# Transposing q and k in fp32, two row tiles at a time, and splitting them into halves behind the transposes

## The chip, the cores and the metric

The kernel runs on one core of a Trainium2 chip. The metric is the device time of one execution in microseconds (us). The core's engines are PE (TensorE, matrix products, with weight loads shown apart as PEld), DVE (VectorE), ACT (ScalarE), POOL (GpSimd) and SP (SyncE, which here only issues transfers). Each engine runs its own queue in order; engines wait for one another through semaphores. Matmul results are written to PSUM, which has eight banks; DVE and ACT read them from there.

## What is computed

An encoder trunk of two layers on 512 rows of 1024 channels, in fp32. Each layer normalises x, projects it (w_in) to q, k and v of two attention branches and to gates, and mixes:

```python
qa = apply_rope(rms_norm(qa.reshape(b, s, HEADS_A, 2, HEAD_DIM), qk_gain_a[l, 0]), cos, sin)
ka = apply_rope(rms_norm(ka.reshape(b, s, HEADS_A, 2, HEAD_DIM), qk_gain_a[l, 1]), cos, sin)
oa = diff_attention(qa, ka, va, lam)             # 8 heads, two softmaxes each, w = p0 - lam * p1
qb = apply_rope(rms_norm(qb...)); kb = ...       # 12 heads in 3 groups of dilated windows
ob = softmax-weighted sum of the three groups' dilated_window_attention
y = (g_a * (oa @ w_branch_a[l]) + g_b * (ob @ w_branch_b[l])) @ w_out[l]
x = x + gate_m * y
h = rms_norm(x, norm_mlp_g[l]) * (1.0 + scale_f) + shift_f
x = x + gate_f * (jnp.square(jax.nn.relu(h @ w_mlp_up[l])) @ w_mlp_down[l])
```

## The kernel before

Products are made in fp32r, a shortened fp32: each fp32 operand is split into a high half (its value rounded to fp32r) and a low half (what is left), and three matmuls (high by high, high by low, low by high) take the place of one. Weight halves are called wh and wl: `split_w` loads `raw`, ACT copies it to wh, and DVE subtracts to get wl.

The 512 rows are four row tiles of 128. The w_in columns are cut into 14 pieces; piece p holds 128 columns each of q, k and v, that is two heads of 64. Pieces 0 to 5 belong to branch B, pieces 6 to 13 to the eight heads of branch A. The main loop runs over slots: slot k multiplies row tile k%4 of piece k//4 (24 matmuls of 384 columns, in three parts, into an `acc` bank), and slots 56 to 61 multiply gates. Between the parts of a slot stands the work of earlier tiles and of attention, written out by hand in the loop (line 836 on). In that loop every engine's order is fixed as the code emits it (`Ordered`, `nosync`). For one row tile of one piece the steps are:

- `post1`, at the start of the next slot: ACT squares (sq) and copies v; DVE sums (ms), multiplies by gain and rotation (y, sw); POOL makes the scale (rs) and applies it to y, a tile of 128x256: q of two heads, then k of two heads.
- `post2`, at the end of the same slot: ACT writes the high halves of q and twice those of k into a tile T of 128x768 (fp32r), and DVE subtracts to get the low halves.
- `turn`, in the middle of slot k+2 (for the first 18 tiles at the start of slot k+3): PE transposes four 128x128 blocks of T into a PSUM bank tp; ACT copies them to q2 and k2.
- `turn_kl`, behind part 2 of that slot: PE transposes T's last block into the free columns of the slot's acc bank; ACT copies its lower 64 partitions to kl and DVE its upper 64.

Per head, q2 holds high and low half on the two partition halves, k2 the high half twice, and kl the low half on one side and zeros on the other, so a score is two matmuls:

```python
matmul(o, q2[:, c, qt], k2[:, c, ks], start=True, stop=False)
matmul(o, q2[:, c, qt], kl[:, c, ks], start=False, stop=True)
```

Attention B has its tiles in slots 14 to 17 and 26 to 29, two to a slot; a tile's e is transposed one slot later (six transposes tp<-e in two banks, copied by ACT to wT). Attention A has head h's four tiles in slots 30+4h to 33+4h. In such a slot, in this order: post1 of the slot before; `leave` (ACT, squares and copies of an earlier head output); `load(0)`; part 0 (9 matmuls); `turn` of the tile two slots back (PE tp<-p, ACT wT); `score` (PE s; DVE the two maxima nm; ACT the exponentials p<-s,nm); `load(1)`; `mix` (DVE r, rho and p<-p,rho); part 1 (9 matmuls); the turn of q and k; `load(2)`; part 2 (6 matmuls); `load(3)`; `value` (PE pv<-v,wT); and at a head's end `out` (PE tp<-identr,o; ACT and DVE oaT). Weight loads of the next piece stand in slots with k%4 == 1 (`load(0)`) and k%4 == 3 (the other three); a head's `out` stands in slots with k%4 == 1, which are the last before a new head's k and q are read (slot 37 is the one after which head 2 starts).

Pools that matter here: tp has two banks used in turn by every transpose; acc has two banks, and three more are shared with the scores, which slots named in WIDE may use too; y has two buffers and T three.

Of the kernel before, what the change touches and what calls it, by code (L numbers as in the profile page):

```python
# [10 lines left out]
F32 = mybir.dt.float32  # L11
R32 = mybir.dt.float32r
BF = mybir.dt.bfloat16
I32 = mybir.dt.int32
AF = mybir.ActivationFunctionType
# [6 lines left out]
KT = 8  # L22
# [19 lines left out]
def trunk(ctx, tc, x, c, pos, cols, rows, ada_w, w_qkv, w_gate, w_ba, w_bb, w_out, w_up, w_down, out):  # L42
# [12 lines left out]
    sp = pool("scr", 2)  # L55
# [33 lines left out]
    T_, V_, S_, G_ = Ordered(nc.tensor), Ordered(nc.vector), Ordered(nc.scalar), Ordered(nc.gpsimd)  # L89
    E_ = Ordered(nc.sync)  # L90
    matmul = T_.matmul
    transpose = T_.transpose
# [9 lines left out]
    tps = lambda: tpp.tile([128, 4, 128], F32, name="tp", tag="tp")  # L102
# [19 lines left out]
    identr = consts.tile([128, 128], R32, name="identr")  # L122
    V_.tensor_scalar(identr, ii, 0.0, None, op0=OP.is_equal)
    ident = identr.bitcast(F32)
# [222 lines left out]
    def qkv(l, p, ab, hT):  # L347

        w, kv, sts = [], [], []

        def outer(kt):
            if kt == 0:
                begin()
                for t in range(NT):
                    pool_, tag = ((ssp, "s"), (ssp, "s"), (ssp, "s"), (pvp, "pv"))[t]
                    sts[t]["ps"] = pool_.tile([128, 512], F32, name="acc", tag=tag)
            wh, wl = w[kt // 2]
            cw = slice(384 * (kt % 2), 384 * (kt % 2) + 384)
            for t in range(NT):
                tk = slice(128 * t, 128 * t + 128)  # L360
                mm3(sts[t]["ps"][:, :384], hT[kt][0][:, tk], hT[kt][1][:, tk], wh[:, cw], wl[:, cw],
                    kt == 0, kt == KT - 1)

        def load(i, spare=False):
            w.append(split_w(w_qkv[l, p, i], 768, spare=spare))

        def begin():
            kv.extend([big([128, 2, 512], R32, "q2"), big([128, 2, 512], R32, "k2"),
                       big([128, 2, 512], R32, "kl"),
                       halfp.tile([128, NT, 128], F32, name="v", tag="half")])  # L370
            G_.memset(kv[2][64:128, 0].bitcast(F32), 0.0)
            G_.memset(kv[2][0:64, 1].bitcast(F32), 0.0)

        def slot(t):
            st = {}
            sts.append(st)
            tk = slice(128 * t, 128 * t + 128)

            def part(k0, k1, f=None):
                if k0 == 0:  # L380
                    if t == 0:
                        begin()
                    st["ps"] = acc(4 * p + t in WIDE[l])
                for kt in range(k0, k1):
                    wh, wl = w[kt // 2]
                    cw = slice(384 * (kt % 2), 384 * (kt % 2) + 384)
                    mm3(st["ps"][:, :384], hT[kt][0][:, tk], hT[kt][1][:, tk], wh[:, cw], wl[:, cw],
                        kt == 0, kt == KT - 1)
                if k1 == KT and f is not None:
                    f(st["ps"][:, 384:512])  # L390

            def post1():
                ps, v = st["ps"], kv[3]
                ps4 = ps[:, :256].rearrange("p (a d) -> p a d", d=64)
                sq = sqs[sqn[0] % 2]
                sqn[0] += 1
                S_.activation(sq[:, :, :64], ps4, AF.Square, scale=0.125)
                S_.activation(v[:, t], ps[:, 256:384], AF.Copy)
                ms = small([128, 4], "ms4")
                rs = small([128, 4], "rs4")  # L400
                V_.reduce_sum(ms, sq, axis=AX.X)
                G_.tensor_tensor(rs, ms, half_neg[:, :4], op=OP.pow)
                y = st["y"] = sp.tile([128, 4, 64], F32, name="y", tag="y")
                g = GT[:, t, 2 * ab:2 * ab + 2][:, :, None].to_broadcast([128, 2, 2, 64])
                V_.tensor_mul(y.rearrange("p (a b) d -> p a b d", b=2),
                              ps4.rearrange("p (a b) d -> p a b d", b=2), g)
                sw = sp.tile([128, 4, 2, 8], F32, name="sw")
                V_.tensor_mul(sw, ps4[:, :, :16].rearrange("p a (h d) -> p a h d", h=2)[:, :, ::-1],
                              ST[:, t, ab].rearrange("p a (h d) -> p a h d", h=2))
                V_.tensor_add(y[:, :, :16], y[:, :, :16], sw.rearrange("p a h d -> p a (h d)"))  # L410
                G_.tensor_mul(y, y, rs[:, :, None].to_broadcast([128, 4, 64]))

            def post2():
                y = st["y"]
                T = sp.tile([128, 12, 64], R32, name="T", tag="T", bufs=3)
                S_.activation(T[:, 0:4:3], y[:, 0:2], AF.Copy)
                S_.activation(T[:, 5:11].rearrange("p (a b) d -> p a b d", a=2)[:, :, 0:2],
                              y[:, 2:4][:, :, None].to_broadcast([128, 2, 2, 64]), AF.Copy)
                V_.tensor_sub(T.rearrange("p (a b) d -> p a b d", a=4)[:, 0:4:3, 1:3],
                              y.rearrange("p (a b) d -> p a b d", a=2),  # L420
                              T.rearrange("p (a b) d -> p a b d", a=2)[:, :, 0:4:3].bitcast(F32))
                st["T"] = T.rearrange("p a d -> p (a d)")

            def turn():
                q2, k2, kl, _ = kv
                T = st["T"]
                tp = tps()
                for i, a in enumerate((0, 128, 320, 512)):
                    transpose(tp[:, i].bitcast(R32), T[:, a:a + 128], identr)
                S_.activation(q2[:, :, tk], tp[:, 0:2], AF.Copy)  # L430
                S_.activation(k2[:, :, tk], tp[:, 2:4], AF.Copy)

            def turn_kl(o):
                transpose(o.bitcast(R32), st["T"][:, 640:768], identr)
                S_.activation(kv[2][0:64, 0, tk], o[0:64], AF.Copy)
                V_.tensor_copy(kv[2][64:128, 1, tk], o[64:128])

            return {"bank": lambda: st["ps"],
                    "parts": [lambda f: part(0, 3), lambda f: part(3, 6), lambda f: part(6, 8, f)],
                    "turn": turn, "kl": turn_kl, "post1": post1, "post2": post2}  # L440

        return {"kv": kv, "load": load, "outer": outer, "slots": [slot(t) for t in range(NT)]}

    last_exp = [None]
# [159 lines left out]
    LAG = 2  # L604
    STRIDE = 2
    WIDE = ([*range(18, 25)], [*range(13), *range(18, 25)])
    POST = 90
    TURN = 18
    FIRST = 0
    AHEAD = 4  # L610
# [115 lines left out]
    for l in range(DEPTH):  # L726
# [67 lines left out]
        done = 0  # L794
        if l == 0:
            done = NT
# [4 lines left out]
        slots = []  # L801
# [16 lines left out]
        nq = 4 * NB_Q  # L818
# [5 lines left out]
            loads.setdefault((k - 1, 1), []).append(slots[k]["load"])  # L824
        mods = {k: 16 + i for i, k in enumerate(range(54, 62))}
        MODS = len(mods)
        post1_at, post2_at, turn_at = {}, {}, {}
        for k in range(nq):
            at = k + 1 if k >= done else STRIDE * k + done + FIRST
            post1_at.setdefault((at, k < done), []).append(slots[k])  # L830
            post2_at.setdefault((at + (k < done), k < done), []).append(slots[k])
            if k < TURN:
                turn_at.setdefault((at + 2 + (k < done), False), []).append(slots[k])
            else:
                turn_at.setdefault((at + 1, True), []).append(slots[k])
        for k in range(done, max(len(slots), max(x[0] for x in due) + 1)):
# [11 lines left out]
            parts = slots[k]["parts"] if k < len(slots) else [lambda f: None] * 3  # L848
            for sl in turn_at.get((k, False), []):
                sl["turn"]()  # L850
                sl["kl"]((sl if sl in slots[:done] else slots[k - 1])["bank"]()[:, 384:512])
            for sl in post2_at.get((k, True), []):
                sl["post2"]()
            for sl in post1_at.get((k, False), []):
                sl["post1"]()
            run((0, "leave"), (1, "leave"))
# [2 lines left out]
            run((0, "turn"), (0, "score"))  # L859
            load(1)  # L860
            run((0, "mix"))
            if k >= POST:
                for sl in post2_at.get((k, False), []):
                    sl["post2"]()
            parts[1](None)
            run((1, "turn"), (1, "score"))
            due_t = turn_at.get((k, True), [])
            for sl in due_t:
                sl["turn"]()
            load(2)  # L870
            parts[2](due_t[0]["kl"] if due_t and k < nq else None)
            if k >= nq:
                for sl in due_t:
                    sl["kl"](tps()[:, 0])
            for sl in post1_at.get((k, True), []):
                sl["post1"]()
            load(3)
            if k < POST:
                for sl in post2_at.get((k, False), []):
                    sl["post2"]()  # L880
            if l == 0 and k in mods:
                ada(0, mods[k])
            run((0, "value"), (1, "value"), (0, "out"), (1, "out"))
# [39 lines left out]
        for cc in range(2):  # L923
# [6 lines left out]
            for t in range(NT):  # L930
                if cc == 0:
                    x1[t] = load_x(t, xsrc)
                ps = acc()
                tk = slice(128 * t, 128 * t + 128)
# [4 lines left out]
                d = sp.tile([128, 512], F32, name="d", tag="f512", bufs=6)  # L939
# [334 lines left out]
```

## Time and profile before

| | |
|---|---|
| median of 3 runs | 1869.1 us (1868.28 to 1869.27) |
| the profiled execution | 1869.08 us, span 1867.3 us |
| granted TensorE clock | 0.999 |
| busy, of the span | PE 99%, PEld 87%, DVE 70%, ACT 55%, POOL 17% |
| main loop of layer 0, of layer 1 | about 76 to 430 us, about 965 to 1350 us |
| mean busy share of the DMA engines, 250 to 410 us | 0.20 |

A profile row of the groups gives line, engine, operation, output<-input with sizes, xcount, then busy us and mean ns of one, then how long the engine had been idle before them and who ended that. A row of the timeline gives start and duration in us. All instructions that pass through the ordering helper carry its line, L81, so they are told apart by the names of their tiles. In the names, buffer numbers are left out (k is k2, q is q2). PE's matmuls overlap, so the distance between starts tells their cost, not the duration.

### The profile page before, as it was taken

To read this page: it belongs to the slowest core of one execution; us is meant where nothing else is said; L and a number is where in the kernel's file an instruction comes from. 1 tells how busy PE (TensorE), PEld (TensorE's weight loads), DVE (VectorE), ACT (ScalarE), POOL (GpSimd) and SP (SyncE) were. 2 spreads that over 40 slices of the span, in tenths; PEclk is the share of its full clock that TensorE was granted. 3 is DMA by queue.
4 is the path that set the end of the run, shared out by engine and by line. 5 is a ranking of instruction groups with operands and counts; after the bars stand their busy time and mean duration, and the time that the engine had idled before them with its cause. 6 is when DMAs were issued, how large, how long until landed. Compare 5 with 4: busy or idle time off the path is not lost.

```text
span 1867.3 us, 27230 instructions
## 1 busy us (share of the span) xinstructions
PE 1839.7 (99%) x9988; PEld 1627.4 (87%) x9988; DVE 1312.9 (70%) x2379; ACT 1022.6 (55%) x2309; POOL 316.2 (17%) x407
## 2 busy tenths in 40 slices
PE   7999999999999999999999999999999999999999
PEld 6999999998888877888889999999888888888887
DVE  8765567777575998777775555777546568778786
ACT  5565567776433544455355555777662345545442
POOL 1332224421121000000034232244110100000000
PEclk9999999999999999999999999999999999999999
DMA  8321111114663663333432121112136635323322
GB/s 331 111 69 53 59 46 57 60 59 153 197 227 117 240 226 109 110 97 111 148 114 77 47 74 43 54 58 71 46 114 214 202 117 167 112 91 102 102 75 83
DMA packets 63639, 212.09 MB, mean 114 GB/s; under 512 B 7185, under 2 KB 7569, under 8 KB 63506
## 3 DMA queue, kind: packets, MB, share of 16 engines
q1 hardware_dynamic: 63218, 210.27, 34.6%
q8 instruction: 79, 1.29, 0.3%
q14 instruction: 54, 0.44, 0.1%
q10 hardware_dynamic: 288, 0.09, 0.0%
HBM read 205.09 MB, written 5.24 MB: 113 GB/s over the span
## 4 chain that ended last, share of the span: by engine, by line
PE 85%; DVE 7%; ACT 5%; POOL 2%; issue 1%; DMA 1%; DVEq 0%; ACTq 0%; POOLq 0%
PE acc L81 72%; PE tp L81 5%; PE s L81 4%; PE pv L81 3%; PE pvb L81 2%; DVE wl L81 2%; DVE raw L81 1%; POOL rs L81 1%; ACT T L81 1%; DVE e L81 1%; ACT e L81 1%; ACT wh L81 1%; POOL y L81 1%; DVE ms L81 1%; DVE y L81 1%
## 5 line engine op out<-in xcount | busy, mean ns | idle before, releaser
L81 PE MATMUL acc<-wh,hT 128*128 128x384 f32 x1792 | 516.1, 345 | 4.5 <-ACT hT L81 3.3
L81 ACT ACTIVATE wh<-raw 128x1024 fp32r<-128x1024 f32 (+1 forms) x331 | 323.7, 988 | 311.2 <-PE acc L81 175.6
L81 DVE TENSOR_TENSOR wl<-raw,wh 128x1024 fp32r<-128x1024 f32 (+1 forms) x331 | 376.7, 1147 | 159.3 <-ACT wh L81 152.5
L81 PE MATMUL acc<-hT,wh 128*128 128x512 f32 (+1 forms) x1632 | 482.2, 379 | 0.4 <-ACT wh L81 0.4
L81 PEld LDWEIGHTS acc<-hT,wh 128*128 128x128 f32 x1632 | 298.5, 188 | 56.3 <-ACT wh L81 1.8
L81 PEld LDWEIGHTS acc<-wh,hT 128*128 128x128 f32 x1792 | 329.3, 188 | 10.6 <-ACT hT L81 4.7
L81 PE MATMUL acc<-hT,wl 128*128 128x512 f32 (+1 forms) x816 | 306.2, 378 | 3.1 <-DVE wl L81 3.1
L81 PE MATMUL acc<-wl,hT 128*128 128x384 f32 x896 | 302.2, 337 | 0.8 <-DVE wl L81 0.8
L81 PE MATMUL acc<-wh,uT 128*128 128x512 f32 (+1 forms) x928 | 291.4, 388 | 2.6 <-DVE y L81 2.5
L81 PEld LDWEIGHTS acc<-wh,uT 128*128 128x128 f32 x928 | 173.8, 188 | 39.0 <-issue 2.9
L81 POOL TENSOR_TENSOR rs<-ms,half_neg 128x4 f32<-128x4 f32 (+1 forms) x128 | 123.7, 966 | 477.1 <-DVE ms L81 475.9
L81 PEld LDWEIGHTS acc<-hT,wl 128*128 128x128 f32 x816 | 153.6, 188 | 32.6 <-DVE wl L81 4.5
L81 PE MATMUL acc<-wl,uT 128*128 128x512 f32 (+1 forms) x464 | 179.6, 387 | 0.0
L81 PEld LDWEIGHTS acc<-wl,hT 128*128 128x128 f32 x896 | 169.0, 189 | 4.9 <-DVE wl L81 1.9
L81 DVE CUSTOM_DVE_ANT_0 raw<-raw,cbc,colt 128x1024 f32<-128x1024 f32 x96 | 123.9, 1300 | 40.3 <-DMA raw<-in_ada_w 40.2
L81 ACT ACTIVATE p<-s,nm 128x512 f32<-128x512 f32 x128 | 86.9, 684 | 62.0 <-DVE nm L81 62.0
L81 DVE TENSOR_TENSOR y<-y,acc 128x512 f32<-128x512 f32 x146 | 96.1, 683 | 13.1 <-PE acc L81 12.8
L81 PEld LDWEIGHTS acc<-wl,uT 128*128 128x128 f32 x464 | 87.1, 188 | 17.8
L81 DVE TENSOR_REDUCE nm<-s 128x1 f32<-128x512 f32 x128 | 82.3, 685 | 28.0 <-PE s L81 27.5
L81 ACT ACTIVATE wT<-tp 128x512 f32<-128x512 f32 (+1 forms) x128 | 65.9, 542 | 46.0 <-PE tp L81 46.0
L81 ACT ACTIVATE T<-y 128x128 fp32r<-128x128 f32 x224 | 68.8, 358 | 38.9 <-POOL y L81 38.8
L81 DVE TENSOR_TENSOR T<-y,T 128x256 fp32r<-128x256 f32 x112 | 51.4, 459 | 52.6 <-ACT T L81 51.6
(156 smaller groups left out, 2734.9 us busy)
## 6 DMA issues: line engine op xcount, KB each, us to landing
raw<-in_ada_w SPq DMA_DIRECT2D x96, 512.0 KB, 4.2
raw<-in_w_qkv SPq DMA_DIRECT2D x112, 384.0 KB, 3.2
raw<-in_w_up SPq DMA_DIRECT2D x64, 512.0 KB, 3.7
raw<-in_w_down SPq DMA_DIRECT2D x64, 512.0 KB, 3.6
raw<-in_w_gate SPq DMA_DIRECT2D x32, 512.0 KB, 3.6
raw<-in_w_ba SPq DMA_DIRECT2D x16, 512.0 KB, 4.3
raw<-in_w_out SPq DMA_DIRECT2D x16, 512.0 KB, 4.0
xt<-in_x SPq DMA_DIRECT2D x8, 512.0 KB, 5.9
```

Of the source, the lines that this page charges most:

```text
L81: ins = f(*a, **k)
```

## The change

`post2`, T and `turn_kl` are gone. y stays in fp32 and has six buffers of its own. `turn` does nothing for even tiles; for an odd tile it transposes y of this tile and the one before it, q and k of both, in four fp32 transposes into one tp bank. Then ACT copies the high halves of q and k to the partition half on which they stand (four copies of 64x256), and for each of the two heads ACT copies k's high half to the other partition half, and DVE subtracts to get q's low half on the other partition half and k's low half in place. When a turn comes due is not changed, except that a pair has its odd tile's time.

```diff
-            def part(k0, k1, f=None):
+            def part(k0, k1):
...
-                if k1 == KT and f is not None:
-                    f(st["ps"][:, 384:512])
...
-                y = st["y"] = sp.tile([128, 4, 64], F32, name="y", tag="y")
+                y = st["y"] = sp.tile([128, 4, 64], F32, name="y", tag="yq", bufs=6)
...
-            def post2():
-                y = st["y"]
-                T = sp.tile([128, 12, 64], R32, name="T", tag="T", bufs=3)
-                S_.activation(T[:, 0:4:3], y[:, 0:2], AF.Copy)
...
-                st["T"] = T.rearrange("p a d -> p (a d)")
-
             def turn():
+                if t % 2 == 0:
+                    return
                 q2, k2, kl, _ = kv
-                T = st["T"]
                 tp = tps()
-                for i, a in enumerate((0, 128, 320, 512)):
-                    transpose(tp[:, i].bitcast(R32), T[:, a:a + 128], identr)
-                S_.activation(q2[:, :, tk], tp[:, 0:2], AF.Copy)
-                S_.activation(k2[:, :, tk], tp[:, 2:4], AF.Copy)
-
-            def turn_kl(o):
-                transpose(o.bitcast(R32), st["T"][:, 640:768], identr)
-                S_.activation(kv[2][0:64, 0, tk], o[0:64], AF.Copy)
-                V_.tensor_copy(kv[2][64:128, 1, tk], o[64:128])
...
+                for i in range(2):
+                    y = sts[t - 1 + i]["y"].rearrange("p a d -> p (a d)")
+                    for j in range(2):
+                        transpose(tp[:, 2 * j + i], y[:, 128 * j:128 * j + 128], ident)
+                tq, tk_ = (tp[:, 2 * j:2 * j + 2].rearrange("p a b -> p (a b)") for j in range(2))
+                both = slice(128 * t - 128, 128 * t + 128)
+                halves_ = (slice(0, 64), slice(64, 128))
+                for c in range(2):
+                    S_.activation(q2[halves_[c], c, both], tq[halves_[c]], AF.Copy)
+                    S_.activation(k2[halves_[c], c, both], tk_[halves_[c]], AF.Copy)
+                for c in range(2):
+                    h, o = halves_[c], halves_[1 - c]
+                    S_.activation(k2[o, c, both], tk_[h], AF.Copy)
+                    V_.tensor_sub(q2[o, c, both], tq[h], q2[h, c, both].bitcast(F32))
+                    V_.tensor_sub(kl[h, c, both], tk_[h], k2[h, c, both].bitcast(F32))
...
-                sl["kl"]((sl if sl in slots[:done] else slots[k - 1])["bank"]()[:, 384:512])
-            for sl in post2_at.get((k, True), []):
-                sl["post2"]()
...
-            parts[2](due_t[0]["kl"] if due_t and k < nq else None)
+            parts[2](None)
```

Three places in the built programs show what moves. The rows name operation, output<-input and size, and in brackets the semaphores that the instruction waits for.

ACT, attention A of layer 0, a slot with three weight loads (k%4 == 3), before, from the transposed p (wT) on; the two exponentials follow it:

```order
L81 ACTIVATE wT<-tp 128x512 [waits PE_49]
L81 ACTIVATE p,sm<-s,nm 128x512 [waits DVE_49] x2
L81 ACTIVATE wh<-raw 128x768 [waits DMAHW6_49]
L81 ACTIVATE q_3732<-tp 128x2x128 [waits PE_49]
L81 ACTIVATE k_3733<-tp 128x2x128
L81 ACTIVATE wh<-raw 128x768 [waits DMAHW7_49]
L81 ACTIVATE kl<-acc 64x128 [waits PE_49]
L81 ACTIVATE wh<-raw 128x768 [waits DMAHW0_49]
L81 ACTIVATE T<-y 128x2x64 [waits Pool_49]
L81 ACTIVATE T<-y 128x2x128
L81 ACTIVATE sq_117<-acc 128x4x64 [waits DVE_49]
```

The same stretch of ACT in the changed program:

```order
L81 ACTIVATE wh<-raw 128x768 [waits DMAHW6_49]
L81 ACTIVATE q_3481<-tp 64x256 [waits PE_49]
L81 ACTIVATE k_3482<-tp 64x256
L81 ACTIVATE q_3481<-tp 64x256
L81 ACTIVATE k_3482<-tp 64x256 x2
L81 ACTIVATE k_3482<-tp 64x256 [waits DVE_49]
L81 ACTIVATE wh<-raw 128x768 [waits DMAHW7_49]
L81 ACTIVATE wh<-raw 128x768 [waits DMAHW0_49]
L81 ACTIVATE sq_117<-acc 128x4x64 [waits PE_49]
```

The copies to T and kl are gone, six copies out of tp stand together, the last of them waits for DVE, and two of the slot's wh stand behind it.

DVE in a slot with k%4 == 1, the last before a head's first scores, before, from the maxima (nm) on:

```order
L81 TENSOR_REDUCE nm<-s 128x1 [waits PE_49] x2
L81 RECIPROCAL r_3933<-sm 128x2 [waits Activation_49]
L81 SCALAR_TENSOR_TENSOR rho<-sm,nlam,r_3933 128x1 [waits DVE_49]
L81 SCALAR_TENSOR_TENSOR p<-p,rho 128x512 [waits DVE_49]
L81 CAST kl<-acc 64x128 [waits Activation_49]
L81 TENSOR_TENSOR T<-y,T 128x2x128 [waits Activation_49,Pool_49]
L81 TENSOR_TENSOR oaT<-tp,oaT 128x512 [waits Activation_49]
L81 TENSOR_REDUCE ms_4273<-sq_117 128x4 [waits Activation_49]
```

The same stretch of DVE in the changed program:

```order
L81 SCALAR_TENSOR_TENSOR p<-p,rho 128x512 [waits DVE_49]
L81 TENSOR_TENSOR q_3481<-tp,q_3481 64x256 [waits PE_49,Activation_49]
L81 TENSOR_TENSOR kl<-tp,k_3482 64x256
L81 TENSOR_TENSOR q_3481<-tp,q_3481 64x256 [waits Activation_49]
L81 TENSOR_TENSOR kl<-tp,k_3482 64x256
L81 TENSOR_TENSOR oaT<-tp,oaT 128x512 [waits Activation_49]
L81 TENSOR_REDUCE ms_3983<-sq_117 128x4 [waits Activation_49,Pool_49]
```

Four subtractions stand where kl and T stood, behind p<-p,rho as those did; the first and the third wait for ACT (the semaphore's values, read in the built program, are those of ACT's fifth and sixth copy out of the bank; the sixth copy's wait is for the second subtraction).

PE across the end of such a slot, before, from the kl transpose through the head's output (tp<-identr,o) to the next slot's first scores:

```order
L81 MATMUL acc<-identr,T 128x128
L81 MATMUL pv<-v,wT 128x128 [waits Activation_49]
L81 MATMUL pv<-v,wT 128x128 x3
L81 MATMUL tp<-identr,o 128x128 [waits PE_49,Pool_49]
L81 MATMUL tp<-identr,o 128x128 x3
L81 MATMUL acc<-wh,hT 128x384 [waits DVE_49]
...
L81 MATMUL tp<-identr,p 128x128 [waits PE_49,Activation_49]
L81 MATMUL tp<-identr,p 128x128 x3
L81 MATMUL s<-k_2993,q_2992 128x512
L81 MATMUL s<-kl,q_2992 128x512 [waits Activation_49]
```

The same end of a slot in the changed program:

```order
L81 MATMUL pv<-v,wT 128x128 x3
L81 MATMUL tp<-identr,o 128x128 [waits PE_49,Pool_49]
L81 MATMUL tp<-identr,o 128x128 x3
L81 MATMUL acc<-wh,hT 128x384 [waits DVE_49]
...
L81 MATMUL tp<-identr,p 128x128 [waits DVE_49,PE_49]
L81 MATMUL tp<-identr,p 128x128 x3
L81 MATMUL s<-k_2794,q_2793 128x512 [waits Activation_49]
L81 MATMUL s<-kl,q_2793 128x512
```

The transpose for kl is gone, and tp<-identr,p now waits for DVE: the bank it takes is the one out of which q and k were split, and the value it waits for is that of the last subtraction.

More of the change, by code (lines that the diff above doesn't have):

```diff
@@ L411, in post1 @@
                 G_.tensor_mul(y, y, rs[:, :, None].to_broadcast([128, 4, 64]))
-            def post2():
-                y = st["y"]
-                T = sp.tile([128, 12, 64], R32, name="T", tag="T", bufs=3)
-                S_.activation(T[:, 0:4:3], y[:, 0:2], AF.Copy)
[L417 to L421, printed above, removed]
-                st["T"] = T.rearrange("p a d -> p (a d)")
@@ L438, in slot @@
-            return {"bank": lambda: st["ps"],
-                    "parts": [lambda f: part(0, 3), lambda f: part(3, 6), lambda f: part(6, 8, f)],
-                    "turn": turn, "kl": turn_kl, "post1": post1, "post2": post2}
+                for i in range(2):
[3 more added lines that the diff above has]
+                tq, tk_ = (tp[:, 2 * j:2 * j + 2].rearrange("p a b -> p (a b)") for j in range(2))
@@ L442, in qkv @@
+            return {"parts": [lambda f: part(0, 3), lambda f: part(3, 6), lambda f: part(6, 8)],
+                    "turn": turn, "post1": post1}
         return {"kv": kv, "load": load, "outer": outer, "slots": [slot(t) for t in range(NT)]}
@@ L606, in trunk @@
     WIDE = ([*range(18, 25)], [*range(13), *range(18, 25)])
-    POST = 90
     TURN = 18
@@ L826, in trunk @@
         MODS = len(mods)
-        post1_at, post2_at, turn_at = {}, {}, {}
+        post1_at, turn_at = {}, {}
         for k in range(nq):
@@ L830, in trunk @@
             post1_at.setdefault((at, k < done), []).append(slots[k])
-            post2_at.setdefault((at + (k < done), k < done), []).append(slots[k])
             if k < TURN:
@@ L861, in trunk @@
             run((0, "mix"))
-            if k >= POST:
-                for sl in post2_at.get((k, False), []):
-                    sl["post2"]()
             parts[1](None)
@@ L870, in trunk @@
             load(2)
-            parts[2](due_t[0]["kl"] if due_t and k < nq else None)
-            if k >= nq:
-                for sl in due_t:
-                    sl["kl"](tps()[:, 0])
+            parts[2](None)
             for sl in post1_at.get((k, True), []):
@@ L877, in trunk @@
             load(3)
-            if k < POST:
-                for sl in post2_at.get((k, False), []):
-                    sl["post2"]()
             if l == 0 and k in mods:
```

## The prediction, made before the changed kernel was timed

> **What bounds the kernel now.** I read three views in this order: the page's busy times, the stage windows, and the timeline of the stretch in which the changed lines run. The engines of the whole span, and layer 0's attention-A stage (160 us of it):
>
> ```profile
> PE 1839.7 (99%) x9988; PEld 1627.4 (87%) x9988; DVE 1312.9 (70%) x2379; ACT 1022.6 (55%) x2309; POOL 316.2 (17%) x407
> ...
> 250.00:410.00 160.00, 160.00 (x1045) 153.45 (x1044) 122.11 (x282) 118.23 (x368) 58.66 (x78) 1.00 0.20 61
> ```
>
> (The second row's columns are the stretch and its length, then busy time of PE, PEld, DVE, ACT and POOL, the clock, DMA's share and GB/s.) PE is never idle in that window at granted clock 1.00, while DVE is busy 76% and ACT 74% of it (122.11 and 118.23 of 160). So a microsecond that leaves PE's queue there is gained, as long as DVE and ACT, whose queues are in order, keep up. The groups that the change removes, reshapes, or is priced by:
>
> ```profile
> L81 ACT ACTIVATE T<-y 128x128 fp32r<-128x128 f32 x224 | 68.8, 358 | 38.9 <-POOL y L81 38.8
> ...
> L81 DVE TENSOR_TENSOR T<-y,T 128x256 fp32r<-128x256 f32 x112 | 51.4, 459 | 52.6 <-ACT T L81 51.6
> ...
> L81 ACT ACTIVATE q<-tp 128x256 fp32r<-128x256 f32 x112 | 42.2, 377 | 32.2 <-PE tp L81 32.2
> ...
> L81 DVE CAST kl<-acc 64x128 fp32r<-64x128 f32 x108 | 31.8, 295 | 54.3 <-ACT kl L81 52.6
> ...
> L81 ACT ACTIVATE kl<-acc 64x128 fp32r<-64x128 f32 x108 | 28.9, 267 | 12.7 <-PE acc L81 12.7
> ...
> L81 DVE TENSOR_TENSOR y<-acc,GT 128x256 f32<-128x256 f32 x112 | 47.3, 423 | 2.8
> ...
> L81 ACT ACTIVATE wT<-tp 128x512 f32<-128x512 f32 x96 | 57.2, 595 | 46.0 <-PE tp L81 46.0
> ```
>
> **PE: the gain.** PE's matmuls overlap, so their cost is the distance between starts. These rows are of slots 35 (274 to 276) and 37 (290 to 292):
>
> ```profile
> 274.34 0.46 PE L81 MATMUL tp<-identr,T 128*128 128x128 f32 x4
> ...
> 274.88 0.34 PE L81 MATMUL acc<-wl,hT 128*128 128x384 f32 x1
> ...
> 275.76 0.22 PE L81 MATMUL acc<-identr,T 128*128 128x128 f32 x1
> 275.76 0.97 PEld L81 LDWEIGHTS pv<-v,wT 128*128 128x128 f32 x8
> ...
> 290.64 0.60 PE L81 MATMUL tp<-identr,o 128*128 128x128 f32 x4
> ...
> 291.25 0.33 PE L81 MATMUL acc<-wl,hT 128*128 128x384 f32 x1
> 291.42 0.52 PE L81 MATMUL acc<-wh,hT 128*128 128x384 f32 x2
> ```
>
> A 384-column matmul takes 0.17 (291.25 to 291.42). From four fp32r transposes to the second matmul behind them is 0.54, so the four cost 0.37. The fifth pushes back the loads of pv by one place; eight of these take 0.97 and the last is 0.19 long, so a place is 0.11. A row tile costs 0.48 and two of them 0.96. The changed kernel has four fp32 transposes for two tiles. Their operand is fp32 like that of tp<-o, which stands ahead of the same matmuls: 0.61 less 0.17, or 0.44. That is 0.52 less for each pair of tiles, and 28 pairs in each of two layers make 29.1 us. Bounds: at the fp32r price (0.37) it would be 33 us; were an fp32 transpose to take double its row (0.88), 4 us.
>
> **ACT and DVE: less work, in another shape.** ACT loses the two T copies (0.72 a tile), q and k (0.38 each) and kl (0.27), 3.5 us a pair, and gets six copies of 64x256. No row has their shape: kl with half the elements is the floor (0.27), wT with double the ceiling (0.60). q has the same elements per partition, and kl on 64 partitions is no faster than its elements ask, so I take 0.38. DVE loses T (0.46) and kl (0.30), 1.5 a pair, and gets four subtractions out of PSUM: floor kl 0.30, ceiling T 0.46, taken from y<-acc, 0.42. As busy time this is covered by PE. POOL and SP issue what they did. Outside the loop PE's order differs in one place of layer 0's MLP, where some acc<-hT matmuls change places with acc<-wh,uT ones; both kinds are there before and after, and I count nothing for it.
>
> What is not covered is the order. The transposed bank is read by both engines, and the built program lets them take turns on it: DVE's first subtraction waits for ACT's fifth copy, ACT's sixth for DVE's second subtraction, DVE's third for the sixth copy. ACT is in order, so behind the sixth copy are held the weight halves (wh) and the next exponentials; and DVE comes to its first subtraction only after p<-p,rho, which ends the slot's softmax. The bank comes free with the last subtraction, and in a slot with k%4 == 1 the output transpose takes the other bank, so the next slot's tp<-p waits for it.
>
> **One head, followed round.** The rows are the same work in slots 35 to 37, and the last but one starts the head's boundary:
>
> ```profile
> 271.41 0.60 PE L81 MATMUL tp<-identr,p 128*128 128x128 f32 x4
> ...
> 272.51 1.29 DVE L81 TENSOR_REDUCE nm<-s 128x1 f32<-128x512 f32 x2 [0.95 <-PE s L81]
> ...
> 274.58 0.84 ACT L81 ACTIVATE wh<-raw 128x768 fp32r<-128x768 f32 x1
> ...
> 275.31 0.38 ACT L81 ACTIVATE q<-tp 128x256 fp32r<-128x256 f32 x1
> ...
> 275.45 0.96 DVE L81 TENSOR_TENSOR wl<-raw,wh 128x768 fp32r<-128x768 f32 x1 [1.66 <-ACT wh L81]
> ...
> 275.58 0.39 ACT L81 ACTIVATE k<-tp 128x256 fp32r<-128x256 f32 x1
> ...
> 276.33 0.16 DVE L81 RECIPROCAL r<-sm 128x2 f32<-128x2 f32 x1
> ...
> 276.77 0.75 DVE L81 SCALAR_TENSOR_TENSOR p<-p,rho 128x512 f32<-128x512 f32 x1
> ...
> 277.44 0.95 DVE L81 TENSOR_TENSOR wl<-raw,wh 128x768 fp32r<-128x768 f32 x1
> ...
> 278.35 0.60 PE L81 MATMUL tp<-identr,p 128*128 128x128 f32 x4
> ...
> 279.96 0.42 DVE L81 TENSOR_REDUCE ms<-sq 128x4 f32<-128x260 f32 x1
> ...
> 280.41 0.42 DVE L81 TENSOR_TENSOR y<-acc,GT 128x256 f32<-128x256 f32 x1
> ...
> 280.75 0.21 DVE L81 TENSOR_TENSOR sw<-acc,ST 128x64 f32<-128x64 f32 x1
> ...
> 281.14 1.28 DVE L81 TENSOR_REDUCE nm<-s 128x1 f32<-128x512 f32 x2
> ...
> 283.80 0.75 DVE L81 SCALAR_TENSOR_TENSOR p<-p,rho 128x512 f32<-128x512 f32 x1
> ...
> 285.66 0.41 DVE L81 TENSOR_REDUCE ms<-sq 128x4 f32<-128x260 f32 x1
> ...
> 287.76 1.28 DVE L81 TENSOR_REDUCE nm<-s 128x1 f32<-128x512 f32 x2
> ...
> 288.22 0.46 PE L81 MATMUL tp<-identr,T 128*128 128x128 f32 x4
> ...
> 289.83 0.38 ACT L81 ACTIVATE q<-tp 128x256 fp32r<-128x256 f32 x1
> ...
> 316.44 0.46 PE L81 MATMUL tp<-identr,T 128*128 128x128 f32 x4
> ```
>
> A head takes 28.22 now (288.22 to 316.44). Prices: a hand-over between engines 0.03 (wh ends 275.42, wl starts 275.45), copies 0.27 apart (275.31, 275.58), subtractions 0.34 (y to sw), wl 0.88 (275.45 to 276.33), p 0.67 (276.77 to 277.44). Round the changed program, from one boundary's tp<-p to the next:
> - PE through slot 38 (6.94 less the 0.48) and to the first maximum of slot 39 (1.10): 7.56.
> - nm to the end of p, with one wh and wl between: 5.01 (272.51 to 277.52).
> - the first hold: two subtractions from 0.08 before that end (0.76), hand-over, the sixth copy (0.27), the held wh (0.84), hand-over, two wl (1.76): 3.61.
> - ms to nm 1.18; nm to the end of p's place 3.33 (2.66 and 0.67); ms to nm with a wl 2.10; nm to the first copy 2.07.
> - the second hold: five copies (1.46), two subtractions, the sixth copy (0.38), two subtractions (0.76 each time), four hand-overs: 3.48.
>
> The sum is 28.34, while PE would need 28.22 less two pairs' gain, 27.18. The round over DVE and ACT is the longer: tp<-p waits about 1.16 us at every boundary, and the head gains nothing. The round has seven copies and six subtractions: at their floors (0.11 and 0.13 shorter) it is 26.8 and PE decides again, at their ceilings (0.22 and 0.04 longer) 30.1.
>
> On the subtractions the Trainium skill can be held against the row ("Perfetto Trace Analysis", Optimizing Scalar/DVE Operations): it puts DVE's overhead at about 60 ns on SBUF and 125 on PSUM. By it a subtraction would cost 65 ns more than T's 0.46 from SBUF; with six of them on the round, ten heads would be an estimated 6 us longer and the whole 1872. The rows have PSUM no dearer (y 423 ns, T 459), and the sum goes by them.
>
> **Outside the heads.** Where pairs are turned at a slot's start and the slot's own tp<-e need both banks, the same hold stands in PE's way, in slots 16 and 18 (layer 1):
>
> ```profile
> 1035.59 1.57 ACT L81 ACTIVATE wh<-raw 128x768 fp32r<-128x768 f32 x2
> ...
> 1038.25 0.44 PE L81 MATMUL tp<-identr,e 128*128 128x128 f32 x2 [0.49 <-ACT k L81]
> ...
> 1057.28 0.39 ACT L81 ACTIVATE q<-tp 128x256 fp32r<-128x256 f32 x1 [1.48 <-PE tp L81]
> ...
> 1058.83 0.82 PE L81 MATMUL tp<-identr,e 128*128 128x128 f32 x6
> ```
>
> The hold of 3.48 starts at 1037.06, when wh lets go: the bank is free at 1040.5 instead of 1038.25, 2.3 us. In slot 18 it starts at 1057.28 and ends at 1060.8; the last two of six transposes would start at 1059.3 (four places of 0.11), so 1.5 us. Per layer 3.8.
>
> **The sum.** Gain 29.1. Given back: the five heads between the boundaries at slots 37 and 57, in each layer, 11.6 (1.04 and 0.12 a head, times ten); the heads' two ends and the slot where they begin (32, 34, 58), where the round is not closed, taken at two thirds of a wait, 4.7; slots 16 and 18, 7.6; in layer 0, where the slots up to 17 have two acc banks, a pair at a slot's start ends its last subtraction 4.1 after it (0.60 for the transposes, then 3.48) and the bank's last reader sw 1.0 later, against a next slot 4.6 on (24 matmuls of 0.17 and 0.44): 0.4 to 0.5 in five slots, 2. Together 25.9, so 3.2 us less than the profiled 1869.08 (its span 1867.3; the median is 1869.1): **1866 us**.
>
> **Rivals.** *The holds are hidden* and PE's gain stays: 1841, or up to 1858 where half of the waits remain. For it: PE has no idle time in the heads now, and DVE loses kl and T in slots without a pair, which the round only counts in part. Against it: the round closes with 0.03 hand-overs and no slack. It decides where the round falls by 1.16, under PE's 27.18. *The hold grows*, on the other side: the T copies show DVE idle 51.6 us behind ACT over 60 waits, so a turn between the engines may cost more than 0.03 where an instruction waits for two semaphores, and a copy across partition halves has no row at all. Half a microsecond more in each of the two holds of a head and the 8 outside is 14 us in ten heads and those slots: 1880. It is slower than before from 0.25 us a hold. *PE saves little*, because an fp32 transpose of y is dearer than one of o: at double the row a pair gains 0.08 instead of 0.52, which takes 15.8 from the 36 pairs outside the ten heads (the heads go by the round): 1882. For it is only that y has no row; it decides against the change from four transposes at about 0.63.
>
> **How the numbers follow.** The forecast's own case, 1859 to 1874, has 0.48; holds hidden 0.23; the hold grows 0.22; PE saves little 0.07. About 0.2% (3.7 us) is what a measurement tells from no change: faster is below 1865.4, slower above 1872.8. Of the forecast's case 0.19 is faster, 0.23 the same, 0.06 slower. With the rivals: faster 0.42, same 0.23, slower 0.35. The range that leaves out the far half of the first rival and the top of the second is 1850 to 1882.
>
> **What would show it.** tp<-identr,y x4 in 0.6 and half as many stretches; k<-tp with a wait for DVE q or kl in each pair; a PE wait of about 1.2 at tp<-p ("<-DVE kl") once a head, and 2.3 and 1.5 at tp<-e in slots 16 and 18; the head at 28.3. If PE shows no wait at tp<-p, the first rival is right; if wh's late halves stop PE at acc<-wl too, the second.

## The result and the profile after

The changed kernel takes 1887.4 us (median of 4 runs, 1886.65 to 1888.87) against 1869.2 (1868.28 to 1869.28): 1.0100 times as long, interval 1.0088 to 1.0112. The forecast was 1866.0 with a range of 1850 to 1882, so it is slower by 18.2 us where slightly faster was forecast. The profiled execution took 1886.65 us, its span 1884.9.

First the page of the changed kernel, its window of layer 0's attention A, its two new groups, and PE's waits over the whole span (us, how often, the longest):

```profile
PE 1824.5 (97%) x9652; PEld 1606.4 (85%) x9652; DVE 1319.5 (70%) x2379; ACT 994.0 (53%) x2085; POOL 318.0 (17%) x407
...
250.00:410.00 160.00, 152.03 (x942) 143.03 (x941) 117.92 (x273) 109.39 (x314) 56.82 (x76) 1.00 0.19 61
...
L81 ACT ACTIVATE k<-tp 64x256 fp32r<-64x256 f32 x224 | 83.7, 374 | 61.9 <-DVE kl L81 61.2
L81 DVE TENSOR_TENSOR q<-tp,q 64x256 fp32r<-64x256 f32 x112 | 47.3, 422 | 87.2 <-ACT k L81 86.8
...
PE tp L81 <- DVE kl L81: 21.5, 18, 3.1
PE acc L81 <- DVE wl L81: 9.3, 17, 1.3
PE acc L81 <- DVE y L81: 4.8, 2, 4.2
```

PE has 15 us less work (1839.7 to 1824.5) and yet the span is 18 longer: of the 160 us in which it was never idle before, it is now idle for 8. ACT stood 61.2 us ahead of its k copies waiting for DVE, DVE 86.8 ahead of its q subtractions waiting for ACT: the turns on the bank. PE waits 18 times, 21.5 us, for the last subtraction (kl) at a transpose.

A head now takes 29.18 instead of 28.22. This is the hold at the end of the slot before a head (layer 0, timeline of the changed kernel; the last row is the next slot's tp<-p):

```profile
322.58 0.37 ACT L81 ACTIVATE q<-tp 64x256 fp32r<-64x256 f32 x1
322.85 0.37 ACT L81 ACTIVATE k<-tp 64x256 fp32r<-64x256 f32 x1
323.23 0.38 ACT L81 ACTIVATE q<-tp 64x256 fp32r<-64x256 f32 x1
323.52 0.75 ACT L81 ACTIVATE k<-tp 64x256 fp32r<-64x256 f32 x2
...
324.30 0.42 DVE L81 TENSOR_TENSOR q<-tp,q 64x256 fp32r<-64x256 f32 x1 [0.31 <-ACT k L81]
324.73 0.42 DVE L81 TENSOR_TENSOR kl<-tp,k 64x256 fp32r<-64x256 f32 x1
325.18 0.38 ACT L81 ACTIVATE k<-tp 64x256 fp32r<-64x256 f32 x1 [0.91 <-DVE kl L81]
325.60 0.43 DVE L81 TENSOR_TENSOR q<-tp,q 64x256 fp32r<-64x256 f32 x1 [0.45 <-ACT k L81]
326.04 0.43 DVE L81 TENSOR_TENSOR kl<-tp,k 64x256 fp32r<-64x256 f32 x1
326.61 0.63 PE L81 MATMUL tp<-identr,p 128*128 128x128 f32 x4 [1.22 <-DVE kl L81]
```

```profile
309.40 0.75 DVE L81 SCALAR_TENSOR_TENSOR p<-p,rho 128x512 f32<-128x512 f32 x1
310.16 0.42 DVE L81 TENSOR_TENSOR q<-tp,q 64x256 fp32r<-64x256 f32 x1
...
311.04 0.38 ACT L81 ACTIVATE k<-tp 64x256 fp32r<-64x256 f32 x1 [1.49 <-DVE kl L81]
...
312.36 1.83 DVE L81 TENSOR_TENSOR wl<-raw,wh 128x768 fp32r<-128x768 f32 x2
...
313.37 0.44 PE L81 MATMUL acc<-wl,hT 128*128 128x384 f32 x1 [0.33 <-DVE wl L81]
314.10 0.41 DVE L81 TENSOR_REDUCE ms<-sq 128x4 f32<-128x260 f32 x1
```

(The second fence is the other hold of the head, in the slot that loads weights. A hold is the time from a pair's first copy or subtraction until what waits behind it goes on.) The order of events is the one forecast, turn by turn. But subtractions start 0.43 apart, each when the one before has ended, and of the copies only those overlap (0.27, 0.29) that keep to a partition half; the others start 0.37 to 0.38 apart. The first fence takes 4.03 from the first copy to tp<-p, where 3.48 was forecast; the second 3.95 from the end of p to ms, where 3.61 was. Behind the held sixth copy the weight halves come late, too, and PE waits 0.33 at acc<-wl once a head.

### The profile page after: what moved, and what is told of

Its sections match the earlier page's. It is cut to its first block, busy times and chain, and to the rows that moved or that the text cites. A ratio compares the mean times of both kernels' runs of the same rounds, so it can differ in the third digit from the quotient of the medians.

```text
span 1884.9 us, 26491 instructions
## 1 busy us (share of the span) xinstructions
PE 1824.5 (97%) x9652; PEld 1606.4 (85%) x9652; DVE 1319.5 (70%) x2379; ACT 994.0 (53%) x2085; POOL 318.0 (17%) x407
## 4 chain that ended last, share of the span: by engine, by line
PE 74%; DVE 12%; ACT 10%; issue 4%; DMA 0%; POOL 0%; DVEq 0%; ACTq 0%; POOLq 0%
PE acc L81 65%; PE tp L81 4%; DVE wl L81 3%; ACT p L81 3%; PE s L81 3%; ACT k L81 2%; DVE kl L81 2%; PE pvb L81 2%; DVE q L81 1%; DVE nm L81 1%; ACT wh L81 1%; DVE raw L81 1%; PE pv L81 1%; ACT q L81 1%; DVE y L81 1%
## 5 line engine op out<-in xcount | busy, mean ns | idle before, releaser
L81 PE MATMUL acc<-wh,hT 128*128 128x384 f32 x1792 | 507.0, 344 | 7.7 <-ACT hT L81 3.6
L81 ACT ACTIVATE k<-tp 64x256 fp32r<-64x256 f32 x224 | 83.7, 374 | 61.9 <-DVE kl L81 61.2
L81 DVE TENSOR_TENSOR q<-tp,q 64x256 fp32r<-64x256 f32 x112 | 47.3, 422 | 87.2 <-ACT k L81 86.8
```

Source lines behind the costliest of these rows:

```text
L81: ins = f(*a, **k)
```

## The experiments

Theory A after this result: a pair holds its bank, and through the turns both engines, longer than forecast, because copies and subtractions that change their partition half don't overlap. Its rival B: the split is simply too much work for DVE and ACT, in whatever order and place.

**The prices by themselves.** Series of four ahead of the kernel's first work, DVE and then ACT for each:

```diff
+    def measure(name, rows_):
+        mo = big([128, 4, 256], F32, name)
+        for i, (o, h) in enumerate(rows_):
+            V_.tensor_sub(mo[o, i], mt[h, :256], mi[h, :256])
+        mo = big([128, 4, 256], F32, name)
+        for i, (o, h) in enumerate(rows_):
+            S_.activation(mo[o, i], mt[h, 256:512], AF.Copy)
```

> The changed kernel with 28 subtractions on DVE and 28 copies on ACT out of one PSUM bank ahead of its first work, each 256 elements per partition, in series of four on: one partition half throughout (msame), read from the lower half and written to the upper (mcross), written to the halves in turn (mout), read from the halves in turn (min), both in turn (mboth), all partitions (mfull), all and half in turn (mmix). Theory A1 (an instruction overlaps the one before it only on the same partitions): in msame, mcross and mfull the starts lie 0.34 apart on DVE and 0.27 on ACT, where both change (mboth) or one changes 0.42 to 0.44 on DVE and 0.37 to 0.39 on ACT. Rival A2 (subtractions of this shape never overlap, whatever their partitions): 0.43 in all series of DVE.

```profile
1.97 1.41 DVE L81 TENSOR_TENSOR msame<-mt,mi 64x256 f32<-64x256 f32 x4
4.63 1.41 DVE L81 TENSOR_TENSOR mcross<-mt,mi 64x256 f32<-64x256 f32 x4
7.74 1.71 DVE L81 TENSOR_TENSOR mout<-mt,mi 64x256 f32<-64x256 f32 x4 [0.27 <-ACT mcross L81]
11.06 1.72 DVE L81 TENSOR_TENSOR min<-mt,mi 64x256 f32<-64x256 f32 x4 [0.62 <-ACT mout L81]
14.39 1.73 DVE L81 TENSOR_TENSOR mboth<-mt,mi 64x256 f32<-64x256 f32 x4 [1.61 <-ACT min L81]
20.43 1.41 DVE L81 TENSOR_TENSOR mmix<-mt,mi 128x256 f32<-128x256 f32 x4 [1.28 <-ACT mfull L81]
...
3.41 1.19 ACT L81 ACTIVATE msame<-mt 64x256 f32<-64x256 f32 x4 [0.52 <-DVE msame L81]
9.48 1.54 ACT L81 ACTIVATE mout<-mt 64x256 f32<-64x256 f32 x4 [1.77 <-DVE mout L81]
```

A row's second number is the four together, three distances and the last one's duration (about 0.41 on DVE, 0.38 on ACT). So the starts lie 0.33 apart on DVE on one half or across halves in one direction, 0.43 where either the input's or the output's half changes; on ACT 0.27 and 0.39. Changing both costs no more than changing one. All partitions and the lower half in turn (mmix) overlap like one half: it is the start partition that counts (0 and 64 were tried), not how many partitions. A1 holds, A2 falls. For DVE the Trainium skill states this rule ("VectorE: DVE Perf Modes", Two Vector instructions with no wait between them): an instruction whose input or output starts in another quadrant than the last one's in the same memory is held until all earlier ones have finished. The series agrees with it, mmix too, and ACT behaves the same way.

**The same work on one half.** Count, order, bank and turns are kept:

```diff
+                h = halves_[0]
...
-                    S_.activation(k2[o, c, both], tk_[h], AF.Copy)
-                    V_.tensor_sub(q2[o, c, both], tq[h], q2[h, c, both].bitcast(F32))
+                    S_.activation(cx[h, c], tk_[h], AF.Copy)
+                    V_.tensor_sub(q2[h, c, both], tq[h], q2[h, c, both].bitcast(F32))
```

> The changed kernel with the same count, order, bank and turns, but all six copies and four subtractions of a pair read and write the lower 64 partitions, so that none changes its half (the upper halves of q2, k2 and kl stay zero and the two cross copies go to a scratch tile: the scores are not the reference's). Theory A1 (what the forecast mis-sized is the overlap: 0.39 instead of 0.27 for a copy, 0.43 instead of 0.34 for a subtraction where the half changes): the hold at a slot's end falls from 4.03 to about 3.5 and the other by 0.3, a head to 28.3 to 28.5, the whole to 1870 to 1878. Rival A2 (the two waits of the turns are what was dearer): a head stays at 29.0 to 29.2 and the whole above 1883.

```profile
315.00 0.42 DVE L81 TENSOR_TENSOR q<-tp,q 64x256 fp32r<-64x256 f32 x1
315.34 0.41 DVE L81 TENSOR_TENSOR kl<-tp,k 64x256 fp32r<-64x256 f32 x1
...
317.08 0.63 PE L81 MATMUL tp<-identr,p 128*128 128x128 f32 x4 [0.64 <-DVE kl L81]
```

1862.9 us, ratio 0.9967 (0.9955 to 0.9980) to the kernel before: 24.5 less than the changed kernel, a larger fall than A1 expected. The subtractions are 0.34 apart, the hold (313.53 to 317.08) is 3.55, and a head takes 28.2 to 28.3. The forecast's prices, which are those of this kernel, gave 3.48, 28.34 and 1866. The 24.5 are not the heads alone: the two stretches of low clock in slot 16, which a later section follows, are missing from this kernel's trace.

**The bank and the turns, one by one and together.** Six copies ahead of four subtractions takes the turns away; a bank of the scores' pool leaves the turns and takes PE's transposes off the held bank:

```diff
                 for c in range(2):
+                    S_.activation(k2[halves_[1 - c], c, both], tk_[halves_[c]], AF.Copy)
+                for c in range(2):
                     h, o = halves_[c], halves_[1 - c]
-                    S_.activation(k2[o, c, both], tk_[h], AF.Copy)
```

> The changed kernel, but a pair's six copies come first and its four subtractions behind them, so that ACT never waits for DVE in a pair. Theory A (a pair holds the transposed bank too long: turns between ACT and DVE, and copies and subtractions that don't overlap when they change partition halves; followed round the changed kernel's trace, a head takes 29.2): without the turns the hold at a slot's end is 0.17 shorter (4.03 to 3.86), and the weight halves behind the sixth copy come 0.42 earlier in slots with k%4 == 3; a head takes 28.6 and tp<-p waits about 0.65 instead of 1.24 once a head, the whole about 1879. Rival B (only the amount of work in the split counts, its order doesn't): 1886 to 1889, tp<-p waits 1.2 as before.

```diff
-                tp = tps()
+                tp = ssp.tile([128, 4, 128], F32, name="tp", tag="s")
```

> The changed kernel, but a pair is transposed into a bank of the pool of the scores (three banks) instead of one of the two banks of tp; copies and subtractions keep their order and their turns. Theory A (what costs is that PE's next transposes want the bank that the pair holds): tp<-p and tp<-e don't wait any more, the round over DVE loses its detour over PE (DVE waited 1.43 for the scores in slot 39), a head takes about 27.75, and the whole is 1862 to 1870; ACT still waits for DVE within a pair. Rival B (DVE and ACT are the bound, and PE will wait at another place, at the scores or the weight halves): a head stays at 28.7 or more and the whole above 1878.

> Both of the earlier edits in one: a pair is transposed into a bank of the scores' pool, and its six copies come ahead of its four subtractions. Theory A (the hold of the bank and the turns are two parts of one loss): a head, 28.73 with copies first and 28.02 with the score bank, comes to 27.4 to 27.6, where PE decides (27.38 with the split from SBUF); the whole 1848 to 1857. Rival B (each edit removes the same wait, so that together they bring no more than the better one): a head at 28.0, the whole 1862 to 1867.

PE's one wait in a head, first in the kernel with copies first, then in the one with the score bank:

```profile
292.97 0.63 PE L81 MATMUL tp<-identr,p 128*128 128x128 f32 x4 [1.29 <-DVE kl L81]
```

```profile
306.82 0.45 PE L81 MATMUL acc<-wl,hT 128*128 128x384 f32 x1 [0.33 <-DVE wl L81]
```

Copies first: 1872.2 (ratio 1.0019, 1.0010 to 1.0028), a head 28.73. The total fell nearly twice as far as expected (15.2, not 8.4), so B's 1886 to 1889 is out, but the wait at tp<-p stayed at 1.29, as B had it, where A expected 0.65: what went is the wait of 0.33 for the weight halves, and the rest of the 0.45 a head was not followed further. Of the 10 us outside the heads 4.8 lie in slots 16 to 18, where PE now waits 1.2 to 2.2 for ACT's wT in place of 2.1 to 3.1 for kl; the rest was not followed either. Score bank: 1865.1 (0.9973, 0.9961 to 0.9984), a head 28.02 (27.75 expected); here the wait at tp<-p is gone and the one for the weight halves stays. Both together: 1855.4 (0.9928, 0.9916 to 0.9941), a head 27.60, and PE waits nowhere in it. Alone the two bring 15.2 and 22.3, together 32.0: two parts of one loss, as A says, and not one wait removed twice.

**Reading the split from SBUF.** Once with both operands of the subtractions in SBUF, the low halves being zero, and once with a whole output, by one more copy:

```diff
-                    V_.tensor_sub(q2[o, c, both], tq[h], q2[h, c, both].bitcast(F32))
+                    V_.tensor_sub(q2[o, c, both], q2[h, c, both].bitcast(F32), q2[h, c, both].bitcast(F32))
```

> The changed kernel, but the four subtractions take both operands from SBUF (the high half less itself), so the low halves of q and k are zero; their count, size and place in DVE's queue stay, but the transposed bank comes free with ACT's sixth copy and neither engine waits for the other inside a pair. Theory A: the waits at tp<-p and at tp<-e of slots 16 and 18 (21.5 us in 18 places) vanish, a head falls to 27.3 to 27.8, and PE's gain shows: 1843 to 1856. Rival B (DVE's queue has become too long by itself, whichever memory it reads): a head stays above 28.5 and the whole above 1874.

```diff
+                f = sp.tile([128, 4, 128], F32, name="f", tag="tf")
+                S_.activation(f, tp, AF.Copy)
-                tq, tk_ = (tp[:, 2 * j:2 * j + 2].rearrange("p a b -> p (a b)") for j in range(2))
+                tq, tk_ = (f[:, 2 * j:2 * j + 2].rearrange("p a b -> p (a b)") for j in range(2))
```

> The changed kernel with one more copy on ACT: the whole transposed bank goes to SBUF in fp32 (128x512, about 0.5 on ACT a pair), and the six copies and four subtractions read that. The output is whole. Theory A: the bank is free after one copy, so the waits at tp<-p and tp<-e vanish as in the run that split from SBUF (1841.5); ACT has 0.5 more a pair, which the exponentials and weight halves behind it see: 1841 to 1850, a head at 27.4 to 27.6. Rival B (ACT becomes the bound, with seven copies ahead of oaT and the weight halves): a head above 28, the whole above 1856.

```profile
308.75 0.59 ACT L81 ACTIVATE f<-tp 128x512 f32<-128x512 f32 x1
309.37 0.42 ACT L81 ACTIVATE q<-f 64x256 fp32r<-64x256 f32 x1
```

The first takes 1841.5 (0.9856, 0.9842 to 0.9869), the second 1846.2 (0.9878, 0.9865 to 0.9892). In both a head takes 27.38 and PE waits nowhere in it, although DVE does the same four subtractions and ACT, in the second, seven copies. B falls: the work fits, the bank did not. In the second the subtractions still start 0.45 apart, so the lost overlap costs nothing once nobody waits for the bank. The second has a whole output and is the fastest such kernel here: 22.7 us below the kernel before, 41 below the change. The bank is free 0.6 after f starts, instead of 4.

**The clock behind a wait.** In slot 16 of layer 1 the changed kernel's PE waits for kl, and this is what follows (the windows' sixth figure after the stretch and its length is the granted clock):

```profile
1047.77 0.45 PE L81 MATMUL tp<-identr,e 128*128 128x128 f32 x1 [3.06 <-DVE kl L81]
```

```profile
1047.80:1051.20 3.40, 3.40 (x12) 3.21 (x13) 2.25 (x8) 0.83 (x2) 2.66 (x4) 0.50 0.05 18
1051.20:1054.60 3.40, 3.40 (x24) 3.28 (x24) 1.03 (x3) 1.46 (x4) 0.00 (x0) 1.00 0.00 0
```

12 matmuls in 3.40 us at clock 0.50, then 24 at 1.00. Filling the wait with matmuls that nothing reads:

```diff
+                    if a == 4 and filler[0] is not None:
+                        o, count = filler[0]
+                        for _ in range(count):
+                            matmul(o, identr, identr, start=False, stop=False)
```

> The changed kernel with idle-time matmuls: 20 of 128x128 in slot 16 and 14 in slot 18 of both layers, into columns of the acc bank that nothing reads, ahead of the tp<-e transposes that wait there for the pair's bank (2.3 and 3.1 us in slot 16, 2.1 in slot 18). Theory C (a wait of that length costs more than itself: the granted clock is 0.5 for 3.41 us from 133.0 and from 1047.8 in the changed kernel's trace, right behind the two waits in slot 16): the clock stays at 1.00 there, the wait shrinks to what the matmuls don't fill, and the two places come out about 1.7 shorter each, 3.4 in all: 1884. Rival D (the low clock is of other origin): it stays at 0.5 there and the time at 1887.

```profile
1040.39 2.43 PE L81 MATMUL acc<-identr 128*128 128x128 f32 x20
...
1043.70 0.41 PE L81 MATMUL tp<-identr,e 128*128 128x128 f32 x2 [0.88 <-DVE kl L81]
```

```profile
1043.70:1047.10 3.40, 3.40 (x24) 3.28 (x24) 2.19 (x8) 1.31 (x4) 2.66 (x4) 1.00 0.02 6
```

The clock stays at 1.00, also in layer 0, and PE is 1.4 and 1.5 earlier behind the two places: C holds, D falls. The whole is 1881.2 (1.0061, 1.0047 to 1.0075), 6.2 less. 2.9 of it is this; another 2.5 is layer 0's MLP, which came out otherwise, and that led to the next run. The Trainium skill ("TensorE: Matmul & The Clock Gate", Part 1) puts the drop to half behind an idle window of about 3.4 us. Here waits of 2.3 (layer 0) and 3.1 were enough, while one of 2.53 in the kernel before (next section) left it at 1.00.

Where the stretches begin says why. In each trace they begin whole multiples of 3.413 us apart: 133.0, 436.8, 706.4 and 1047.8 in the changed kernel are 89, 79 and 100 of them apart. So what counts is how a wait falls into windows of this length, which the waits don't move. The 3.06 lies in one window, of which PE was idle 0.90; the 2.53 of the kernel before is divided between two, idle 0.22 and 0.52. The run of the prices has the changed kernel's loop some 17 us later, and there the two waits of layer 0 change parts. These are its waits in slots 16 and 18, and the clock behind each:

```profile
150.79 0.41 PE L81 MATMUL tp<-identr,e 128*128 128x128 f32 x2 [2.26 <-DVE kl L81]
173.50 0.41 PE L81 MATMUL tp<-identr,e 128*128 128x128 f32 x2 [2.06 <-DVE kl L81]
...
150.79:154.20 3.41, 3.40 (x24) 3.29 (x24) 2.19 (x8) 1.32 (x4) 2.66 (x4) 1.00 0.00 1
173.78:177.19 3.41, 3.41 (x14) 3.31 (x13) 0.81 (x4) 0.38 (x1) 1.62 (x2) 0.50 0.00 0
```

In the changed kernel it is slot 16's wait (2.27) that lies in one window and is followed by 0.50, and slot 18's (2.06) that is divided and isn't. In the loops and MLPs of all these traces, a window at full clock of which PE was idle 0.56 or more was always followed by one at 0.50, and one of 0.46 or less never.

**The MLP's place.** At the swapped matmuls in layer 0's MLP, PE waits 2.53 before and 4.24 in the changed kernel (the first row is the wait before, the second the changed kernel's clock from within its wait on):

```profile
695.56 0.47 PE L81 MATMUL acc<-wh,uT 128*128 128x512 f32 x1 [2.53 <-DVE y L81]
```

```profile
706.43:713.26 6.83, 4.54 (x11) 3.60 (x12) 6.83 (x10) 2.12 (x2) 0.00 (x0) 0.50 0.51 156
```

The clock is 0.50 for 6.83 us there; before it stayed at 1.00. The edit is the idle matmuls of the last run, now ten of them in slot 16 of layer 0 alone, on top of the evicting kernel:

> The kernel that evicts the whole bank, with ten idle matmuls of 128x128 in slot 16 of layer 0 (into columns of the acc bank that nothing reads), which make the builder put layer 0's MLP matmuls in the order of the kernel before (58 acc<-wh,uT and acc<-wl,uT in a row, then 2 and 12, instead of 52, 2 and 18). Theory E (the swap of matmuls in the MLP, which the forecast counted at nothing, costs time: in the evicting kernel's trace PE waits 4.2 there for y and the clock is 0.5 for 6.8 us from 684.8, in the kernel that split from SBUF, which has the order of before, 2.2 and 3.4): the wait falls to 2.2 to 2.6, the stretch of low clock to 3.4 or none, and the whole from 1846.2 to 1843 to 1845, the ten matmuls' 0.6 to 1.1 us taken off. Rival F (the swap is neutral, and the wait for y comes with the time at which the MLP starts): 1846 to 1848.

```profile
PE acc L81 <- DVE y L81: 3.5, 1, 3.5
```

1846.3 (0.9881, 0.9865 to 0.9898): no change. With the order of before the wait is 3.5 and the clock still 0.50 for 6.83 us from 685.6; PE is 0.6 earlier behind it. Theory E falls. What sets the length of that wait (2.2 to 4.3 in these kernels) stays open.

## Why the prediction was wrong

Where the 17.6 us between the two profiled executions arose, from the same matmuls in both traces: the ten heads from slot 37 to slot 57's output +12.0 (forecast +1.2), slots 16 to 18 +9.9 (forecast 7.6 less four pairs' gain of 2.1, so +5.5), layer 0's MLP +2.1 (forecast 0), all the rest -6.4 (forecast -9.9).

- **The step that failed** is the price list of the round: "copies 0.27 apart", "subtractions 0.34 (y to sw)", and p 0.67 to what follows. Those rows are of neighbours that start on the same partition, and every subtraction of the change, and half of its copies, starts elsewhere than its neighbour. At 0.43 and 0.39 the holds are 0.55 and 0.34 longer (0.11 of the 0.55 is the last hand-over, to PE, which takes 0.14 and not 0.03), and the round, with 0.05 less elsewhere, is 29.18 instead of 28.34. The run on one half shows that this term, with what hangs on it, turns the sign: 24.5 us, more than the whole miss of 21.4. The ceilings in the text (0.60 a copy, 0.46 a subtraction) did cover the true prices; with them the round was given as 30.1. The choice of the nearest row by size, and not by partitions, was the mistake.
- **Right:** the mechanism. The turns on the bank, the held weight halves, the wait at tp<-p once a head (1.16 forecast, 1.22 to 1.30 measured at four of the five boundaries of each layer, 0.4 at the last, and 0.33 more at acc<-wl), the places in slots 16 and 18 (2.3 and 1.5 forecast; 3.1 and 2.1 in layer 1). tp<-y x4 takes 0.60 as forecast, the copies 0.37 to 0.38, the subtractions 0.42.
- **PE's gain** was put 0.10 a pair too high for the heads: in the kernels without a wait a head is 0.83 shorter (28.21 to 27.38), 0.42 a pair and not 0.52. Which of the prices in it is too high stays open. Outside the heads it was not too high: with the split from SBUF, slots 20 to 24 give 0.48 and about 0.6 for their two pairs in either layer, and that kernel is 27.5 faster than the one before, against the forecast's gain of 29.1. PE saves little, the rival, is out.
- **The second rival** is what happened: "the hold grows", with 1880 at half a microsecond a hold. Of its two grounds, the dearer hand-over was not the cause: hand-overs measured 0.03 to 0.04, and 0.14 only to PE. The other was: that a copy across partition halves has no row, which holds for the subtractions as well. The 0.22 it had was too little for a list of prices of which no row had the shape.
- **Not in the sum:** PE's clock. 133.0, 436.8, 706.4 (twice as long) and 1047.8 are stretches at 0.50 that the kernel before hasn't; each of the two that were taken away was worth 1.4 to 1.5. The one at 436.8 follows waits of 1.24 and 1.02 for the weight halves; it lies in the last of layer 0's five heads, which is 3.1 longer than before, where the other nine are about 1.0 longer.

## What to carry to other kernels

On DVE and ACT, an instruction that starts on another partition than its neighbour costs its whole duration (0.43 and 0.39 here), not the distance of overlapping ones (0.33 and 0.27): price a split across partition halves by durations. A PSUM bank from which two engines read in turns is held for all their work, and whoever needs the bank next waits for the last reader; one copy of the whole bank to SBUF first, though more work, made this change worth 22.7 us instead of a loss of 18. And where PE has no slack, a wait of 2 to 3 us can cost about half as much again behind it, if it leaves PE idle for more than about half of one of the clock's windows of 3.41 us.

## What the hardware showed that had not been expected

- On DVE and on ACT a change of the input's or the output's start partition undoes the overlap with the instruction before: 0.33 to 0.43 us and 0.27 to 0.39 us for 256 elements out of PSUM. Reading one half and writing the other, always in the same direction, is free.
- The granted clock falls to 0.50 by windows of 3.41 us that the kernel does not move, and not by the length of a wait: in the loops and MLPs of these traces every window of which PE was idle 0.56 or more was followed by one at 0.50, and none of 0.46 or less from full clock. So waits of 3.1 us and more always brought it, one of 2.53 didn't, one of 2.06 did in one run and not in another, and two of 1.24 and 1.02 close together (434 to 437 in the changed kernel) did.
